# Pinning side work behind the instruction emitted ahead of it

## The chip, the cores and the metric

The kernel runs on one core of a Trainium2 chip. The core has five engines with one instruction queue each: TensorE (PE in the profile) for matrix products, VectorE (DVE) and ScalarE (ACT) for elementwise work, GpSimd (POOL) for a little of it, and SyncE (SP), which issues nearly all transfers. An engine works through its queue in order; between engines semaphores carry the waits. The metric is device time in microseconds (us) of one launch.

## The reference

One inference step of a hybrid decoder layer, for a prompt of 1024 tokens and for 8 sequences of 4 new tokens (32 "sample" rows), at width 1024:

```python
h = rmsnorm(x, g_norm) * (1 + scale) + shift              # shift, scale, gate from silu(c) @ w_ada
mq, mk, mv, mi, mf, mo, mz, aq, ak, av, az, gm, ga = split_in(h @ w_in)
y_m, C, n, m = mlstm_branch(mq, mk, mv, mi, mf, mo, mz, ...)   # 4 heads, chunks of 128, a 128x128 state C per head
q, k = partial_rope(aq), partial_rope(ak)
y_a = sliding_window_attention_with_sinks(q, k, av) * silu(az)  # 8 heads, 2 key/value heads, window 128
u = sigmoid(gm) * (y_m @ w_mo) + sigmoid(ga) * (y_a @ w_ao)
x = x + gate * (u @ w_o)                                   # then a last rmsnorm
```

Outputs are the normalised rows, the mLSTM states and the key/value caches of both parts, all in 32-bit floats.

## The kernel before, in words

Products are made at 32-bit precision from pairs: each operand is split into a high part (`..h`, `wh_..`, a cast on ACT) and a low part (`..l`, `wl_..`, a subtraction on DVE), and three products are added in PSUM. Large products go by a seven-product scheme on halves (`block_products`, `att_products`, `Rows`), whose operands are sums and differences of blocks (`t1` to `t4`, `s1`).

The main chain is written as a plain sequence of jobs: the first products of keys and values (`pair`), the queries (`queries`, whose evacuation `ev_q`, line 886, copies each piece out of PSUM on ACT as `aq`, applies rope on DVE and stores `aqr`), the first mLSTM projections (`head_jobs`), then `block_products` for the other projections and all gates, `att_products` for the attention's output product, the memory branch's output (`mem_out`) and the last product by rows (`Rows`).

Beside it run streams of side work, as Python generators: `unit` (line 814, one attention unit: scores, a maximum `mx`/`nmx`, exponentials, `den`, transposes `pt`, output `oT`), `gates` (596), `head` (1026: the mLSTM of one head, with `prep`, 1043, which masks the loaded `et` and scales `qw`, and `stage_b`, 1080, the chain of states C), `sample_head` (1160, which ends with two transposes `sty` and their evacuation `gs`), `sum_blocks` (1310, sums of the blocks of `x`), `ada_gate` (1917), `out_weights` (1941, products and sums of `w_out` rows, stored as `woD`) and `att_sums` (1587: loads `yr`, takes differences, splits them into `ym_l`/`ym_h` and `ya..`, the operands of `att_products`).

The class `Side` decides when a step of a stream is emitted. It keeps an estimate of PE's clock (`now`, moved on by every product), and after each product of the main chain `tick` steps every stream whose pause is over and whose PSUM bank is free. So the order in which instructions are emitted interleaves main and side work by planned times.

The order emitted isn't the order run. Products always keep it (`in_order`, on every `matmul` and `transpose`). `V`, `S` and `G` wrap VectorE, ScalarE and GpSimd; while `on` is true each of their instructions is tied to the one before it in its wrapper. From line 1913, where the first products are done, to line 2188, where the last rows begin, `V.on` and `S.on` are false, and the framework's scheduler may put an instruction of DVE or ACT ahead of others that were emitted before it, where data allow and where its own estimate says that it is ready earlier. A transfer is issued on SP in the order that the scheduler gives, behind what it waits for; a wait in a queue holds up everything behind it.

In the trace all wrapped instructions have line 220, products 259, transposes 264 and transfers 247; tiles tell them apart.

## Time and profile before

| | |
|---|---|
| median of 3 runs | 839.07 us (838.8 to 839.33) |
| profiled execution | 838.28 us, of which the span is 836.5 us |
| PE busy | 812.5 us, 97% |
| DVE busy | 595.0 us, 71% |
| ACT busy | 420.1 us, 50% |
| mean granted clock of PE | 0.993 |

The page names an instruction by line, engine, operation and "out<-in". A number in brackets at the end of a timeline row is the idle time of the engine just before it and what ended that; in the list of waits the three numbers are total, count and longest. Times are from the start of the span.

### The profile page before, as it was taken

Reading aid. Unit: us, or ns where it says so; the run is one execution under the profiler, and the core shown is the slowest. Engines: PE = TensorE matmul, PEld = TensorE weight load, DVE = VectorE, ACT = ScalarE, POOL = GpSimd, SP = SyncE. Lnnn points to the kernel's source line nnn. Section 1 sums busy time; section 2 is a strip of 40 time slices with the busy share of each in tenths; the row PEclk is TensorE's granted clock in tenths of the full one; section 3 lists DMA queues with packets and bytes.
Section 4 is the critical chain, followed back from the end, with each engine's and each line's share of the span. In section 5 each row is a group of like instructions: output and inputs, shape, how many; then the busy total and the mean of one; then the engine's idle time right before and its main releaser. Section 6 shows DMA issues by size and latency. Waiting matters only on the chain.

```text
span 836.5 us, 15032 instructions
## 1 busy us (share of the span) xinstructions
PE 812.5 (97%) x5129; PEld 670.9 (80%) x5129; DVE 595.0 (71%) x1479; ACT 420.1 (50%) x1030; POOL 67.4 (8%) x128
## 2 busy tenths in 40 slices
PE   6999999999999999999799999999999999999996
PEld 3779897888788788888688877787788789997775
DVE  4889886656655556475575886797668988974776
ACT  4664365655474564545445454444346654334343
POOL 0120000000000001000001010000002104250000
PEclk9999999999999999999899999999999999999998
DMA  9997766346436335388654354464236785643532
GB/s 337 373 356 233 203 188 201 118 156 210 140 111 196 104 107 174 112 271 292 228 175 167 106 178 138 156 203 141 99 93 191 239 291 180 214 134 131 201 107 108
DMA packets 106689, 153.96 MB, mean 184 GB/s; under 512 B 20448, under 2 KB 54368, under 8 KB 106580
## 3 DMA queue, kind: packets, MB, share of 16 engines
q1 hardware_dynamic: 100964, 142.25, 52.1%
q10 hardware_dynamic: 4176, 6.56, 2.3%
q0 software_dynamic: 1472, 4.20, 1.3%
q8 instruction: 40, 0.66, 0.3%
q14 instruction: 37, 0.30, 0.1%
HBM read 109.22 MB, written 44.75 MB: 184 GB/s over the span
## 4 chain that ended last, share of the span: by engine, by line
PE 91%; DVE 4%; DMA 2%; ACT 1%; issue 1%; SPq 1%; DVEq 0%; ACTq 0%
PE bx L259 11%; PE bw L259 11%; PE by L259 11%; PE g_aq L259 6%; PE bz L259 6%; PE g_w_mo L259 5%; PE g_mq L259 3%; PE foW L259 3%; PE foX L259 3%; PE foY L259 2%; PE smp L259 2%; PE oT L259 2%; PE foZ L259 2%; PE sc L259 2%; PE pt L264 2%; PE g_ak L259 1%
## 5 line engine op out<-in xcount | busy, mean ns | idle before, releaser
L220 ACT ACTIVATE p<-p,nmx 128x256 f32<-128x256 f32 (+1 forms) x64 | 31.0, 485 | 13.0 <-DVE nmx L220 12.7
L259 PE MATMUL g_aq<-h_h,wh_aq 128*128 128x384 f32 (+1 forms) x96 | 32.2, 336 | 0.0
L220 DVE CUSTOM_DVE_ANT_0 p<-sc,cst,sink 128x256 f32<-128x256 f32 (+1 forms) x64 | 26.2, 464 | 6.9 <-PE sc L259 6.8
L259 PE MATMUL g_aq<-h_h,wl_aq 128*128 128x384 f32 (+1 forms) x96 | 30.9, 322 | 0.0
L259 PE MATMUL g_aq<-h_l,wh_aq 128*128 128x384 f32 (+1 forms) x96 | 30.8, 321 | 0.0
L259 PE MATMUL g_w_mo<-ym_l,wh_w_mo 128*128 128x384 f32 (+1 forms) x96 | 30.8, 321 | 0.0
L259 PE MATMUL g_w_mo<-ym_h,wh_w_mo 128*128 128x384 f32 (+1 forms) x96 | 30.8, 321 | 0.0
L259 PE MATMUL g_w_mo<-ym_l,wl_w_mo 128*128 128x384 f32 (+1 forms) x96 | 30.8, 321 | 0.0
L247 POOL DMA_DIRECT2D oD<-uqv x16 | 8.9, 554 | 183.4 <-ACT uqv L220 183.4
L220 ACT ACTIVATE et<-et,an 128x128 f32<-128x128 f32 x32 | 11.2, 397 | 19.5 <-DVE et L220 19.3
L220 DVE COPY p<-pt 128x512 f32<-128x512 f32 (+1 forms) x16 | 10.5, 655 | 13.7 <-PE pt L264 13.7
L259 PEld LDWEIGHTS g_aq<-h_h,wh_aq 128*128 128x128 f32 x96 | 18.0, 188 | 2.6 <-issue 1.5
L259 PEld LDWEIGHTS g_w_mo<-ym_l,wh_w_mo 128*128 128x128 f32 x96 | 18.0, 188 | 0.0
L259 PEld LDWEIGHTS g_aq<-h_l,wh_aq 128*128 128x128 f32 x96 | 18.0, 188 | 0.0
L259 PEld LDWEIGHTS g_w_mo<-ym_h,wh_w_mo 128*128 128x128 f32 x96 | 18.0, 188 | 0.0
L259 PE MATMUL sc<-ukv,uqv 64*128 64x256 f32 (+1 forms) x128 | 18.0, 390 | 0.0
L259 PEld LDWEIGHTS g_w_mo<-ym_l,wl_w_mo 128*128 128x128 f32 x96 | 18.0, 188 | 0.0
L259 PEld LDWEIGHTS g_aq<-h_h,wl_aq 128*128 128x128 f32 x96 | 18.0, 188 | 0.0
L220 DVE TENSOR_TENSOR et<-et,cst 128x384 f32<-128x384 f32 (+1 forms) x12 | 6.1, 512 | 16.5 <-DMA et<-nmd 16.5
L264 PE MATMUL pt<-cst,p 128*128 128x128 f32 x120 | 16.4, 277 | 1.1 <-DVE mx L220 1.1
L259 PE MATMUL g_mq<-h_h,wh_mq 128*128 128x384 f32 (+1 forms) x48 | 16.8, 349 | 0.3 <-ACT mk L220 0.3
L220 ACT ACTIVATE sq<-rows_h 128x512 f32<-128x512 f32 (+2 forms) x14 | 8.2, 582 | 17.7 <-issue 12.0
(2073 smaller groups left out, 2848.0 us busy)
## 6 DMA issues: line engine op xcount, KB each, us to landing
x<-xT SPq DMA_DIRECT2D x16, 256.0 KB, 5.4
early_h<-w_ada SPq DMA_DIRECT2D x8, 512.0 KB, 9.1
adar_ga<-w_ada SPq DMA_DIRECT2D x16, 256.0 KB, 4.0
wr_ga<-w SPq DMA_DIRECT2D x16, 256.0 KB, 2.5
wr_gm<-w SPq DMA_DIRECT2D x16, 256.0 KB, 3.3
taD<-gt SPq DMA_DIRECT2D x16, 256.0 KB, 2.2
tmD<-gt SPq DMA_DIRECT2D x16, 256.0 KB, 4.8
wor<-w_out SPq DMA_DIRECT2D x16, 256.0 KB, 3.9
```

Of the source, the lines that this page charges most:

```text
L220: ins = f(*args, **kw)
L247: ins = (eng or nc.sync).dma_start(out, in_)
L259: in_order(nc.tensor.matmul(out, lhsT, rhs, start=start, stop=stop, skip_group_check=more))
L264: in_order(nc.tensor.transpose(out, in_, idn))
```

## The change

`Side.step` marks the two wrapped engines as `late` while a side stream emits a step. Each wrapper remembers the instruction that it emitted last (`before`), main or side. While `on` is false, an instruction emitted in a side step gets an order tie to that last one; an instruction of the main chain gets none. So a side instruction keeps its place behind the instruction emitted just ahead of it on its engine, and main instructions may still be moved ahead of others. GpSimd isn't in the list of engines.

```diff
     def step(self, item):
+        for e in self.engines:
+            e.late = True
         try:
             lag, banks = next(item[0])
             item[1:] = self.now + lag, banks
...
+        for e in self.engines:
+            e.late = False
...
             def __init__(self, eng, name):
-                self.eng, self.name, self.on = eng, name, True
+                self.eng, self.name, self.on, self.late, self.before = eng, name, True, False, None
...
                     ins = f(*args, **kw)
+                    i = getattr(ins, "ins", ins)
                     if self.on:
                         in_order(ins, self.name)
+                    elif self.late and self.before is not None:
+                        no_sync(i, [self.before])
+                    self.before = i
                     return ins
...
+        side.engines = V, S
```

More of the change, by code (lines that the diff above doesn't have):

```diff
@@ L118, in __init__ @@
     def __init__(self, each, limits, quiet):
-        self.each, self.free = each, {}
+        self.each, self.free, self.engines = each, {}, ()
         self.now, self.last, self.quiet, self.products = 0.0, 0.0, quiet, 0
```

## The prediction

> **What bounds the kernel now.** I read the page's first part, then PE's own waits, then a table of stretches, and last the instructions around each place that the change moves.

> ```profile
> span 836.5 us, 15032 instructions
> PE 812.5 (97%) x5129; PEld 670.9 (80%) x5129; DVE 595.0 (71%) x1479; ACT 420.1 (50%) x1030; POOL 67.4 (8%) x128
> ...
> PE xc L259 <- ACT xsq L220: 6.4, 1, 6.4
> PE S L259 <- DVE C L220: 5.5, 1, 5.5
> PE pt L264 <- DVE mx L220: 1.1, 1, 1.1
> ...
> 405.50:411.00 5.50, 0.04 (x2) 0.00 (x1) 1.44 (x4) 0.90 (x4) 0.00 (x0) 0.81 0.95 275
> 411.60:415.70 4.10, 4.10 (x12) 3.33 (x12) 2.67 (x6) 3.16 (x12) 0.10 (x1) 0.50 0.67 228
> 416.00:420.00 4.00, 4.00 (x47) 3.25 (x46) 2.17 (x4) 1.50 (x4) 0.00 (x0) 1.00 0.40 135
> ```

> PE is busy 97% of the span, so the time is PE's work plus PE's waits; what VectorE (DVE) and ScalarE (ACT) do costs nothing until PE waits for it. PE's list of waits shows one large one behind the start: 5.5 us, for DVE's C. In the table of stretches (columns: length, busy time of PE, its weight loads, DVE, ACT, POOL, then the granted clock, DMA share, GB/s) this wait has a second price: for the 4.1 us after it PE's clock is 0.50, which loses 4.1 x 0.5 = 2.05 us more. The span is 836.5 us, the profiled execution 838.28 us, and the median of the runs 839.07 us, 0.8 us more; I add what I find to the median.

> **What moves.** In the built order of the changed kernel PE and POOL have exactly the order of before. DVE, ACT and SP differ. A side instruction can no longer run ahead of what was emitted before it; a main instruction may still pass side work. So each effect is one of two: a side operation that used an early gap now stands late, or a main operation now stands in front of a side operation that PE needs. I went through the new DVE and ACT order with the durations and landings of the trace, and asked at each changed place when PE's operand would be there against when PE took it. Four places come out late or early by over 1 us.

> **Place 1, the query projections (106 to 123 us): costs 4.6 us.**

> ```profile
> 68.38 0.67 DVE L220 TENSOR_TENSOR x<-x,x 128x512 f32<-128x512 f32 x1
> ...
> 105.66 0.48 ACT L220 ACTIVATE aq<-g_aq 128x384 f32<-128x384 f32 x1
> 106.72 0.62 ACT L220 CAST wh_mq<-wr_mq 128x512 fp32r<-128x512 f32 x1 [0.57 <-PE g_aq L259]
> ...
> 106.65 0.34 PE L259 MATMUL g_aq<-h_h,wh_aq 128*128 128x384 f32 x1
> ...
> 110.52 0.12 DVE L220 TENSOR_TENSOR den<-den,nmx 128x4 f32<-128x4 f32 x1
> ...
> 111.84 0.17 DVE L220 TENSOR_TENSOR mr<-mr,row 1x32 f32<-1x32 f32 x1
> ...
> 111.65 0.91 ACT L220 ACTIVATE p<-p,den 128x256 f32<-128x256 f32 x2 [0.87 <-DVE den L220]
> 112.47 0.47 ACT L220 ACTIVATE aq<-g_aq 128x384 f32<-128x384 f32 x1
> ...
> 121.70 0.48 ACT L220 ACTIVATE aq<-g_aq 128x384 f32<-128x384 f32 x1
> ...
> 122.50 0.34 PE L259 MATMUL g_mq<-h_h,wh_mq 128*128 128x384 f32 x1
> ```

> First, on ACT, the second `wh_mq` cast now stands ahead of the `aq` copy of 105.66. The cast waits for PE to release its granule and begins at 106.72 whatever else happens, so the copy begins at about 107.26 (0.54 behind, the cast's 0.62 overlapping it a little): 1.6 us late, done at 107.74. PE needs the bank it frees at 106.65 and waits 1.1 us. Second, on DVE, the attention's `den` of 110.52 now stands behind the gate chain (`mr`, 111.84) and behind three dependent sums of `sum_blocks`, the `x` adds, which ran at 68 to 72 us and now come directly ahead of it. `mr` is itself 1.9 us late through the first step and ends near 113.9; three adds at 0.67 bring `den` to 115.9, 5.4 us late. On ACT the `p` scaling waits for `den` (the row names it) and the `aq` copy of 112.47 stands behind it, now near 117.6. The row of rope, score, exponential and `aq` copy that follows is a closed circle between the two engines and carries about 4.9 us on: the `aq` copy of 121.70 ends at 127.07 instead of 122.18. PE's first `g_mq` product takes that bank: 127.1 against 122.50, 4.6 us in all, the 1.1 us included (second stall about 3.45 us). No other work covers it, since PE's order is fixed. Until 165 us the later places are late by 4.2 us at most against PE's old times, so they disappear in this shift.

> Small ones in between: PE's 1.1 us wait for `mx` (at 291 us) is absorbed by the shift, and about +0.7 us appears near 191 us, where a copy of transposed `p` stands behind two sums of the blocks. I take -0.4 together (-1.5 to +1).

> **Place 2, the large wait: gains 3.9 us and the clock's 2.05 us.**

> ```profile
> 396.39 3.19 SPq L247 DMA_DIRECT2D woDb<-wor  x3
> ...
> 402.60 0.38 SPq L247 DMA_DIRECT2D hk<-kD  x1
> 403.51 0.42 SPq L247 DMA_DIRECT2D et<-nmd  x1
> ...
> 409.50 0.56 DVE L220 TENSOR_TENSOR et<-et,cst 128x384 f32<-128x384 f32 x1 [6.06 <-DMA et<-nmd]
> 410.12 0.56 DVE L220 TENSOR_TENSOR qw<-qw,hq 128x384 f32<-128x384 f32 x1
> 410.60 0.34 DVE L220 SCALAR_TENSOR_TENSOR C<-C,dec,U 128x129 f32<-128x129 f32 x1
> ...
> 411.00 1.22 PE L259 MATMUL S<-hq,hk 128*128 128x128 f32 x4 [5.46 <-DVE C L220]
> ```

> The third link of head 2's C chain stands behind head 3's `et`, which waits for its load; PE waits for the link to free a bank. In the changed order it still stands there: both are side work, emitted in that order. What moves is SP. Three stores of scaled `w_out` rows (`woDb`, 396.39 on, waiting for DVE's products) stood ahead of the head's loads; the products are now done later, their stores come behind these loads, and `et` is issued near 399.4 instead of 403.51, 4.1 us earlier. With the same 6.0 us to landing it is there at 405.4, the link ends near 406.9, and PE, which came at 405.54, waits about 1.4 us plus or minus: 5.5 - 1.4 = 4.1, of which I take 3.9 since place 1 shifts PE and DVE unequally. Such a short wait leaves the clock alone, so the 2.05 us go too. Bounds: the wait vanishes (-5.5 - 2.05 = -7.5), or the load lands as late against PE as before (0).

> **Place 3, the sample heads' transposes (586 us): costs 2.0 us.**

> ```profile
> 586.22 0.25 DVE L220 TENSOR_SCALAR gs<-sty,vec 128x32 f32<-128x32 f32 x1
> 586.39 0.68 DVE L220 TENSOR_TENSOR wl_phead_gate__6931<-ws,wh_phead_gate__6930 128x512 fp32r<-128x512 f32 x1
> 587.00 0.69 DVE L220 SCALAR_TENSOR_TENSOR hg<-hg,hg1z 128x512 f32<-128x512 f32 x1
> ...
> 587.78 0.68 DVE L220 TENSOR_TENSOR ws<-wr_mz,wr_mz 128x512 f32<-128x512 f32 x1
> ...
> 586.52 0.24 PE L264 MATMUL sty<-cst,sz 32*128 32x32 f32 x1 [0.77 <-DVE gs L220]
> ```

> PE's second `sty` waits for the first `gs`. Now three main operations stand ahead of `gs`: `wl_phead_gate`, `ws`, `hg`, at 0.61 from start to start (586.39 to 587.00). 3 x 0.61 = 1.8, and `ws` starts behind a wait for its operand: 2.0. PE has nothing else to do, its order being fixed. Between 1.8 and 2.1.

> **Place 4, the sums of the attention output (651 to 657 us): costs 3.4 us.**

> ```profile
> 651.34 0.68 DVE L220 TENSOR_TENSOR yr<-yr 128x512 f32<-128x512 f32 x1
> 651.95 0.68 DVE L220 TENSOR_TENSOR hg<-p,bw 128x512 f32<-128x512 f32 x1
> 652.54 1.19 DVE L220 TENSOR_TENSOR yr<-yr 128x512 f32<-128x512 f32 x1
> 653.65 0.68 DVE L220 TENSOR_TENSOR ym_h<-yr,ym_l 128x512 fp32r<-128x512 f32 x1
> ...
> 660.38 0.41 DVE L220 TENSOR_TENSOR wl_ao0C<-wr_ao,wh_ao0C 128x256 fp32r<-128x256 f32 x1
> 660.72 0.41 DVE L220 TENSOR_TENSOR wl_ao0D<-wr_ao,wh_ao0D 128x256 fp32r<-128x256 f32 x1
> ...
> 655.80 0.39 PE L259 MATMUL az<-ym_h,wh_ao0A 128*128 128x512 f32 x1
> 656.03 0.39 PE L259 MATMUL az<-ym_l,wl_ao0A 128*128 128x512 f32 x1
> 656.54 0.50 PE L259 MATMUL aw<-yat2h,wh_ao0B 128*128 128x512 f32 x1
> ```

> PE takes `ym_h` (a side product: `yr` difference, then split) at 655.80; it was ready at 654.33. Seven half-size main operations of the next weights (`wl_ao0B`, `wr_ao`, two `wl_ao0C`, a `ws`, two `wl_ao1A`) now run ahead of the `yr` of 651.34: 7 x 0.34 (660.38 to 660.72) = 2.4. Two `hg` operations that came behind and one that came behind the first `yr` add 3 x 0.6 = 1.8, and the queue is already 1.0 to 1.5 late here for the same reason. Together 5.2 for `ym_h`, which ends at 659.5: 3.7 us after 655.80. PE's old spacing of 0.51 at 656.54, against 0.23 before it, held 0.28 us of waiting that is absorbed: 3.4. From here PE runs without a gap to the output products, so all of it reaches the end. Bounds 1.5 (scheduling slack that I do not see) to 4.

> **The sum.** 4.6 - 0.4 - 3.9 - 2.05 + 2.0 + 3.4 = +3.6 us: 841.9 in the profile, 842.7 for the median.

> **Rivals.** (a) Place 2 gives nothing: the trace has DMA share 0.95 in that wait, so an earlier issue could land no sooner. Then +3.6 + 5.95 = +9.6, 848.6. Against it: half the wait was queueing on SP, which the rows show. (b) The clock falls at place 1. The 405.50:411.00 row has a mean of 0.81, so half the clock for 0.38 of 5.5 us: it fell 3.4 us after PE stopped. A stall of 3.45 us is on the edge of that, and would add up to 2.05: 844.8. [...] (c) Faster: side work has slack that swallows delays before they reach PE, at places 1 and 4, the only ones where the delay travels through several instructions. Place 1 then costs only its first step, 1.1, and place 4 its floor, 1.5: 1.1 - 0.4 - 5.95 + 2.0 + 1.5 = -1.75, 837.3. It decides if `den` comes less than 1.1 us late (0.32 us of margin lies between the `aq` copy's end at 122.18 and PE at 122.50, and 0.87 us of ACT's wait for `den` can be given up without harm if `p` comes later too). DVE's 71% speaks for it; against it, each link of the circle in the rows begins where the one before ends. (d) The moves cancel: place 1 at half its price, 840.4.

> **Chances.** Forecast 0.50 (840.8 to 845.5), (a) 0.12, (b) 0.13, (c) 0.12, (d) 0.13. A measurement of this kernel tells 0.2%, 1.7 us, from no change. Slower: forecast, (a), (b) and 0.02 of (d): 0.77. Within 0.2%: the rest of (d) and a third of (c): 0.15. Faster: the rest of (c): 0.08. The range, 838.5 to 847.5, leaves out (a) and (c).

> **What would show it.** Right: in PE's waits a line for `g_mq` behind ACT's `aq` of 3 to 4 us near 123 us; the wait of S for C under 2.5 us with the clock at full speed behind it; `sty` behind `gs` of 2.5 to 3 us in its longest; `az` behind `ym_l` or `ym_h` of 2 to 4 us. Wrong: no PE wait near 123 us, or the 5.5 us wait still there with its slow clock.

## The result and the profile after

The changed kernel takes 850.52 us, median of four runs (847.62 to 852.60), against 839.20 us (838.80 to 840.21) for the kernel before in the same comparison: 1.0131 times as long, 95% interval 1.0099 to 1.0162, so 11.3 us more. The profiled execution is the fastest of the four, 847.62 us with a span of 845.8 us; that of before took 838.28 us. The two traces therefore explain 9.3 us; the other 2 us lie in the runs that were not profiled, and come back below.

First the page of the changed kernel, then its list of TensorE's waits (total, number, longest).

```profile
span 845.8 us, 15020 instructions
PE 814.8 (96%) x5129; PEld 673.1 (80%) x5129; DVE 596.2 (70%) x1479; ACT 418.4 (49%) x1030; POOL 67.2 (8%) x128
...
PE xc L269 <- ACT xsq L224: 6.4, 1, 6.4
PE g_mq L269 <- ACT aq L224: 3.3, 1, 3.3
PE S L269 <- DVE C L224: 3.1, 1, 3.1
PE sty L274 <- DVE gs L224: 3.0, 2, 2.7
PE az L269 <- ACT ym_l L224: 2.2, 1, 2.2
PE sc L269 <- DVE p L224: 1.2, 1, 1.2
PE g_aq L269 <- ACT aq L224: 1.0, 1, 1.0
```

Busy times are those of before within 0.4%; what is new are waits, and half clock behind some of them. The four places of the forecast are all in this list: `g_mq` and `g_aq` (place 1), `S` (place 2, 5.5 us before), `sty` (place 3), `az` (place 4). What the forecast did not have stands in the table of stretches. These are the changed kernel's, cut at the edges of its half-clock stretches (columns as in the prediction; the seventh number is the granted clock).

```profile
124.72:128.13 3.41, 1.46 (x9) 1.16 (x11) 2.35 (x6) 2.36 (x8) 0.00 (x0) 1.00 0.80 257
128.13:131.54 3.41, 3.41 (x13) 2.84 (x10) 2.50 (x8) 1.36 (x4) 0.00 (x0) 0.50 0.65 223
196.40:199.81 3.41, 2.24 (x11) 1.34 (x11) 2.05 (x7) 0.78 (x3) 0.00 (x0) 1.00 1.00 320
199.81:203.22 3.41, 3.41 (x38) 2.73 (x37) 2.26 (x9) 0.76 (x2) 0.00 (x0) 0.50 0.83 245
411.44:414.85 3.41, 1.83 (x17) 1.59 (x15) 0.56 (x1) 1.73 (x8) 0.10 (x1) 1.00 0.65 221
414.85:418.26 3.41, 1.92 (x10) 1.68 (x11) 1.84 (x4) 1.17 (x4) 0.00 (x0) 1.00 0.71 251
418.26:421.68 3.42, 3.42 (x45) 2.79 (x43) 1.98 (x3) 2.21 (x5) 0.00 (x0) 1.00 0.72 253
588.93:592.34 3.41, 0.74 (x3) 0.62 (x4) 2.83 (x6) 0.92 (x2) 0.00 (x0) 1.00 0.00 0
592.34:595.75 3.41, 3.41 (x10) 2.62 (x9) 0.00 (x0) 0.00 (x0) 0.00 (x0) 0.50 0.00 0
```

After the waits of `g_mq`, `sc` and `sty` the clock is 0.50 for one stretch of 3.41 us each. After the 3.1 us wait of `S` it stays at 1.00. The slow stretches begin whole multiples of 3.413 us apart (199.81 - 128.13 = 71.68 = 21 x 3.413; 592.34 - 199.81 = 392.53 = 115 x 3.413): in this trace the edges lie on one grid, and the clock of a stretch goes with TensorE's busy time in the grid stretch ahead of it: 1.46 and 0.74 us of work were followed by 0.50. The wait of `S` is cut by an edge into two halves, each with over 1.8 us of work, and no slow stretch follows it. The stretch ahead of 199.81, with 2.24 us of work, does not fit this and is taken up at the end. Behind `az` the clock stayed at 1.00 as well, with 1.78 us of work in the stretch that holds most of the wait:

```profile
660.61:664.02 3.41, 1.78 (x8) 1.13 (x6) 3.38 (x7) 1.61 (x4) 0.51 (x1) 1.00 0.40 128
664.02:667.44 3.42, 2.64 (x10) 1.97 (x11) 3.35 (x5) 2.62 (x5) 1.10 (x1) 1.00 0.96 299
```

Laying each TensorE instruction's start in one trace beside its start in the other gives this account of the profiled executions, in us:

| where | forecast | measured |
|---|---|---|
| place 1, `g_aq` and `g_mq` | +4.6 | +4.6 |
| `sc` near 191 us / `mx` at 291 us | -0.4 together | +1.2 / -0.5 |
| place 2, wait of `S` | -3.9 | -2.5 |
| place 2, half clock that goes | -2.05 | -2.2 |
| place 3, `sty` | +2.0 | +1.9 |
| place 4, `az` | +3.4 | +2.5 |
| half clock behind `g_mq`, `sc`, `sty` | none | +1.6, +1.4, +1.5 |

The measured column sums to 9.5, within 0.2 of the 9.3. The other runs had still lower clocks: at 847.62, 850.41, 852.60 and 850.63 us the four were granted 0.991, 0.989, 0.987 and 0.989 of the full clock, which is at most 7.6, 9.3, 11.1 and 9.3 us lost ((1 - clock) x span, which also counts slow time in which TensorE waits). Three of these differ from the first by one or two stretches of 1.7 us (half of 3.41). The kernel before is granted 0.993 in most runs, 5.9 us lost. Of the 11.3 us between the medians some 3.4 (9.3 - 5.9) are clock and some 8 are waits; since the clock is on record to 0.001, or 0.85 us, this split is an estimate.

### The profile page after: what moved, and what is told of

Read it like the earlier page. It is cut to its first block, busy times and chain, and to the rows that moved or that the text cites. A ratio compares the mean times of both kernels' runs of the same rounds, so it can differ in the third digit from the quotient of the medians.

```text
span 845.8 us, 15020 instructions
## 1 busy us (share of the span) xinstructions
PE 814.8 (96%) x5129; PEld 673.1 (80%) x5129; DVE 596.2 (70%) x1479; ACT 418.4 (49%) x1030; POOL 67.2 (8%) x128
## 5 line engine op out<-in xcount | busy, mean ns | idle before, releaser
L224 ACT ACTIVATE p<-p,den 128x256 f32<-128x256 f32 (+1 forms) x32 | 14.2, 489 | 11.4 <-DVE den L224 11.4
L224 DVE TENSOR_TENSOR et<-et,S 128x384 f32<-128x384 f32 (+1 forms) x12 | 6.1, 510 | 15.9 <-PE S L269 14.3
```

Source lines behind the costliest of these rows:

```text
L224: ins = f(*args, **kw)
```

## The experiments

All ratios are to the kernel before, run beside each kernel on the same chip. In each diff, the lines are against the kernel named.

**One stage at a time.** Three kernels tie side work in one stage only: `first` until the first projections are done (`products_done`, at about 200 us), `gates` from there to the last query gate, `last` behind it. Against the changed kernel:

```
first:   products_done.append(True)
       + side.engines = ()
gates: - side.engines = V, S          (at the start; set behind products_done)
       + side.engines = ()
         def hook(n, i):
       +     if n == len(paired) + KT:
       +         side.engines = ()
last:  - side.engines = V, S          (at the start)
       + side.engines = ()
         def hook(n, i):
       +     if n == len(paired) + KT:
       +         side.engines = V, S
```

> Side work is tied only until the key/value products are done (to about 200 us); behind that it is free as before. Theory (the loss is made of single waits of TensorE, each with its stage, and of half-clock stretches that follow them): g_mq waits about 3.3 us behind aq, sc about 1.2 us behind p, two half-clock stretches of 3.4 us follow them at 1.5 us each, and the wait of S for C is the one of before, 5.5 us, with its two half-clock stretches: TensorE is 8 to 8.5 us late at 200 us and stays so, about +8 us to the kernel before (847). Rival (the loss is spread over the kernel by engines that hold each other up): about a quarter of the loss of 11 us, +3 us. Rival of the prediction's own sum (stalls without the clock): +5 to +6 us (845).

> Side work is tied only between the end of the key/value products and the end of the query gates (about 200 to 430 us). Theory: the only large change there is the wait of S for C, which falls from 5.5 to about 3.1 us, and the half-clock stretches behind it, worth 2.2 us, which go: -4.7 us to the kernel before (834.5), faster than both kernels. Rival (the clock falls behind any wait of 3 us): -2.5 to -3 us (836.5). Rival (the gain at this place came only because the earlier loss had already given C time): 0 us (839).

> Side work is tied only behind the query gates (from about 430 us). Theory: sty waits 2.7 us behind gs (+1.9), a half-clock stretch follows (+1.5), az waits some 2.4 us behind ym_l and ym_h: +5 to +6 us (845), with one half-clock stretch more than the kernel before. Prediction's own sum without the clock: +4 to +4.5 us (843.5). Rival (spread loss): +5.5 us too, but with many small waits in place of the two.

`first` took 848.41 us (1.0120, 1.0101 to 1.0138), `gates` 834.60 (0.9949, 0.9933 to 0.9966), `last` 846.46 (1.0099, 1.0078 to 1.0121), against 838.93. That is +9.5, -4.3 and +7.5, together +12.7 where the whole change costs 11.3; the difference is within the intervals, some 1.5 us on each term. The loss adds up from its stages, and in each of them TensorE's list has the waits named above and not many small ones. `gates` came near its expectation, though with one half-clock stretch left behind `S`, where none was expected. `first` and `last` each came out about 1.5 us or more above what was expected of them. The profiled execution of `last`, at 849.52 us the slowest of its four, shows what the clock can add:

```profile
659.87:663.28 3.41, 1.42 (x7) 0.74 (x5) 3.41 (x7) 1.41 (x3) 0.72 (x1) 1.00 0.42 127
663.28:666.70 3.42, 2.64 (x6) 1.82 (x7) 3.32 (x6) 2.83 (x5) 0.89 (x1) 0.50 0.87 280
666.70:670.11 3.41, 3.41 (x10) 2.65 (x9) 2.30 (x4) 0.89 (x2) 0.39 (x1) 0.50 0.84 301
```

Here place 4, whose `az` wait was 2.8 us and lay largely in one grid stretch (1.42 us of work), was followed by two slow stretches; in the changed kernel's profile the same wait had none. The other three runs of `last`, 846.04 to 846.70 us at a clock of 0.992 instead of 0.988, lost about two stretches less. So this does not explain why the median lies above the expectation; that stays open.

**What place 1 consists of.** `no_x` ties all streams but the block sums and attention sums. `skip_x` in addition does not tie other side work behind an instruction of that stream. Against the changed kernel:

```
no_x:   - e.late = True
        + e.late = item not in self.streams["x"]["live"]
skip_x: + if self.mark:               (False while a step of stream x runs)
        +     self.before = i
```

> All streams of side work are tied but that of the block sums and the attention sums (x). Theory: without the three block sums ahead of den the wait of g_mq behind aq shrinks from 3.3 us to 1 us or less and its half-clock stretch goes, sc behind p and az behind ym_l go; sty behind gs and its half-clock stretch stay (+3.4), S behind C keeps its gain (-4.7): 0 to +2 us to the kernel before (839 to 841), so 9 to 11 us under the changed kernel. Rival (the gate chain alone, not the block sums, makes g_mq late): g_mq still waits 2 to 3 us, +4 to +5 us.

> As no_x, and the other side work is not tied behind an instruction of the x stream either (it is tied behind the last one that is not of x). Theory (sc waits because the copy of p stands tied behind a block sum that waits for its load): the wait of sc for p and its half-clock stretch go, 1.5 + 1.3 us less than no_x, the wait of g_mq stays at about 1.8 us: 839 to 840. Rival (sc's wait comes from the order on ScalarE, where the scaling of p stands behind a copy of os): as no_x, 842.

`no_x` took 842.21 us (1.0045, 1.0026 to 1.0063) and `skip_x` 841.63 against 838.71 (1.0034, 1.0022 to 1.0047). In `no_x` TensorE is 2.0 us late at `g_mq` instead of 4.6 (its longest wait there is 1.8 us, where 1 or less was expected), `g_aq` no longer waits and `az` no longer waits: the ties of this stream make 2.6 us of place 1 (the sums ahead of `den`) and all of place 4 (the attention sums). The gate chain, most of which VectorE still runs ahead of the scaling of `p`, is the likely rest; no run frees it alone. The changed kernel's VectorE shows the chain that was forecast, with the three sums in one row:

```profile
113.22 0.18 DVE L224 TENSOR_TENSOR mr<-mr,row 1x32 f32<-1x32 f32 x1
113.33 2.12 DVE L224 TENSOR_TENSOR x<-x,x 128x512 f32<-128x512 f32 x3
115.37 0.15 DVE L224 TENSOR_TENSOR den<-den,nmx 128x4 f32<-128x4 f32 x1
```

`sc` still waited in `no_x`, against what was expected of it. On VectorE of `no_x`:

```profile
193.60 0.69 DVE L224 TENSOR_TENSOR hb<-hb,hb 128x512 f32<-128x512 f32 x1 [2.32 <-DMA wr_mq<-w]
194.21 0.55 DVE L224 COPY p<-pt 128x384 f32<-128x384 f32 x1
```

The copy of `p` is itself tied behind a block sum, which comes after 2.32 us of idle time; the releaser named is the transfer that the profile saw last. Freeing the sums alone does not free the copy. In `skip_x` the copy runs ahead of the sum and `sc` does not wait. So the place is the one the prediction named near 191 us, at 1.2 to 1.5 us instead of 0.7. The median fell by only 0.6 us, and not by the 2.8 expected: in the profiled execution of `skip_x` `g_mq` waits 2.3 us and the mean clock is 0.993, against 1.8 us and 0.995 in that of `no_x`, and the two intervals overlap.

**What place 2 consists of.** `pool` is the kernel before with the stores of the scaled `w_out` rows on POOL's queue; `g_only` is `gates` with only stream g tied.

```
pool:   - store(woD[name, k], t)
        + store(woD[name, k], t, nc.gpsimd)
g_only: - e.late = True
        + e.late = item in self.streams["g"]["live"]
```

> The kernel before, the stores of the scaled w_out rows moved from SP's queue to POOL's; the order on TensorE and ScalarE stays, on VectorE one wor product and one wl_pgate change places. Theory (the gain at 405 us comes from the three woDb stores that no longer stand ahead of the head's loads on SP): et<-nmd is issued some 3 to 4 us earlier, the wait of S for C falls to 2 to 3 us: -2.5 to -5 us (835 to 836.5). Rival (the gain comes from VectorE's or ScalarE's order, or the load lands no sooner because the DMA engines are full): the wait stays at 5 to 6 us, 0.

> In the same stage as gates (200 to 430 us), only the scaling of the w_out rows (stream g) is tied; all other side work is free as before. In the kernel before, five of its wor products run on VectorE at 394.5 to 399.2 us ahead of the main product gt, and SP's store taD waits for gt with the head's loads behind it. Theory (the gain at this place is that VectorE order: gt earlier, so the store and the loads behind it earlier): et<-nmd goes out some 3 us earlier against TensorE, the wait of S for C is 2.5 to 3.5 us and one half-clock stretch instead of two: -4 us (835), as gates. Rival (other side work's ties make the gain): 0 to -1 us.

`pool` took 840.92 us against 838.71 (1.0042, 1.0023 to 1.0060), with `S` waiting 6.1 us and a new wait of 1.2 us of `bw` for `ws`. `g_only` took 834.35 against 838.75 (0.9949, 0.9932 to 0.9967), as much as `gates`. The stores on SP were not what made the load late. In `pool`, first on VectorE and then on SP:

```profile
401.05 0.68 DVE L220 TENSOR_TENSOR gt<-p,bw 128x512 f32<-128x512 f32 x1
...
402.42 0.32 SPq L247 DMA_DIRECT2D taD<-gt  x1
...
405.44 0.42 SPq L247 DMA_DIRECT2D et<-nmd  x1
```

With the `woDb` stores gone, SP issues nothing from 397.1 to 402.42 us: it stands at the store of the main product `gt`, and `gt` comes late because VectorE runs four `wor` products of the side work ahead of it (four, not the five of the expectation). In the kernel before the same two rows lie at 399.15 (`gt`) and 400.53 us (`taD`), with `et` at 403.51. In `g_only` `gt` runs after one `wor`, at 397.13, and `et` is issued at 401.08 us:

```profile
397.13 0.68 DVE L224 TENSOR_TENSOR gt<-p,bw 128x512 f32<-128x512 f32 x1
...
406.95 0.56 DVE L224 TENSOR_TENSOR et<-et,cst 128x384 f32<-128x384 f32 x1 [3.24 <-DMA et<-nmd]
407.94 0.56 DVE L224 TENSOR_TENSOR qw<-qw,hq 128x384 f32<-128x384 f32 x1 [0.43 <-DMA qw<-wid]
```

**What the wait of `S` is made of.** `link` is the kernel before with `et` and `qw` ordered behind the last link of the C chain on VectorE; `gates_link` and `g_link` add the same to `gates` and `g_only`.

```
+ e = V.tensor_tensor(et[:, :m], et[:, :m], cmask..., op=ALU.add)
+ no_sync(getattr(e, "ins", e), links[-1:])
  ...                                           (the same for qw)
+ l = V.scalar_tensor_tensor(Cn, chain[-1], dec..., Un[:, i], ...)
+ links.append(getattr(l, "ins", l))
```

> The kernel before with one order more on VectorE: et and qw of a head come behind the last link of the C chain, so that the third link no longer stands behind a load. Theory (the wait of S for C is that link's place and nothing else): the wait of 5.5 us goes, and with it both half-clock stretches: -6.5 to -7.5 us (832). Rival (VectorE still stands at et until 409.5 us, and the next gate weights behind et come late now that TensorE comes earlier): a new wait of 2 to 4 us for a wl_pgate or for et, -3 to -5 us (835). Rival (S waits for the load in another way too): 0.

> gates with the order of link added: et and qw behind the last C link on VectorE. Theory (two costs in series at one place: the third link behind et, which link takes away, and the late load, which holds VectorE's et and ScalarE's exp with the copies behind it, which gates makes 3 us earlier): S no longer waits, the copies hv and hk come in time, no half-clock stretch: -7 to -8 us to the kernel before (831.5), 3 us under gates. Rival (the copies behind the exp are still late): smpo waits for hv 0.5 to 1.5 us, -5.5 to -6.5 us (833).

> g_only with the order of link added. Theory: as gates_link, -7 to -8 us (831.5), if g_only gives what gates gives. Rival: -3 us, as link alone.

`link` took 835.64 us (0.9962, 0.9948 to 0.9976): its rival's figure. `S` no longer waits, so the third link behind a load was indeed the whole wait. But `smpo` and `smp` now wait 1.6 and 1.4 us for ScalarE's copies `hv` and `hk`, which stand behind the exponential of the same late `et`:

```profile
409.67 0.40 ACT L220 ACTIVATE et<-et,an 128x128 f32<-128x128 f32 x1 [7.42 <-DVE et L220]
```

The 5.5 us wait had hidden that second queue. With both repaired, `gates_link` took 829.55 us (0.9889, 0.9874 to 0.9904), 2 us below what was expected of it, and `g_link` 831.32 (0.9920, 0.9896 to 0.9944), where `smp` still waits 1.1 us. TensorE's waits in `gates_link`, all over 0.2 us:

```profile
PE xc L269 <- ACT xsq L224: 6.8, 1, 6.8
PE sty L274 <- DVE gs L224: 1.1, 2, 0.8
PE adat_q L269 <- ACT adas_q L224: 0.7, 1, 0.7
PE xc L269 <- ACT xsum L224: 0.7, 1, 0.7
PE bw L269 <- ACT bw L224: 0.7, 1, 0.7
PE pt L274 <- DVE mx L224: 0.5, 1, 0.5
PE g_mq L269 <- ACT mk L224: 0.3, 1, 0.3
```

This kernel is 9.2 us faster than the kernel before and by the distances to it (9.2 and 11.3) some 20 us faster than the changed one.

**Place 3 by itself.** `swap` is the changed kernel with both `sty` transposes ahead of both `gs` products.

```
  for i, (g, _) in enumerate(tails):
      tr(ty[:, i], ns[:, i, 0:128], ident[:NS, :NS])
+ for i, (g, _) in enumerate(tails):
      V.tensor_scalar(gs[:, g], ty[:, i], gmn[:, g:g + 1], None, op0=ALU.mult)
```

> The changed kernel, with both sty transposes emitted ahead of both gs products, so that the second no longer waits for the first gs; nothing else moves. Theory: the 2.7 us wait and its half-clock stretch go, and nothing takes their place: TensorE gains 2.5 us against the changed kernel plus up to 1.5 us of clock: 847 to 848. Rival (gs is needed soon after by someone else): a wait of 1 to 2 us some us later, 849.5.

It took 846.41 us against 838.75 (1.0089, 1.0073 to 1.0105), 3.6 us less than the changed kernel by their medians' distances to the kernel before (7.7 against 11.3). `sty` is gone from TensorE's waits, and the runs were granted 0.989 to 0.993 of the clock, against 0.987 to 0.991 in the changed kernel's. No new wait took its place in that stage; `az` further on waited 2.8 us in the profiled execution, against 2.2 in the changed kernel's.

**The clock by itself.** `fill` is the changed kernel with nine products that nobody uses between the two `sty` transposes; `fill_S` is the kernel before with sixteen ahead of `S`.

```
fill:   + if h == 3 and not i:
        +     warm = po([128, 128], "warm")
        +     for _ in range(9):
        +         in_order(nc.tensor.matmul(warm, ident, ident, start=True, stop=True))
fill_S: + if h == 2 and p == 2:
        +     for _ in range(16):
        +         in_order(nc.tensor.matmul(tv[:, 2], ident, ident, start=True, stop=True))
```

> The changed kernel with nine products of a 128x128 unit matrix, used by nobody, on TensorE between the two sty transposes, where it waits 2.7 us for gs. The wait for gs ends at the same time. Theory (a half-clock stretch follows a stretch in which TensorE was idle too long): with TensorE busy in most of the wait no half-clock stretch follows at 590 us, so TensorE's lateness grows by 1.9 us there and not by 3.4: about 1.5 us less where the changed kernel has that stretch, 849 for the median. Rival (the slow clock comes from something else that goes on at this place, as the DMA traffic or the power drawn by what follows): the half-clock stretch is there as before, 850.5.

> The kernel before, with sixteen products of a unit matrix, used by nobody, on TensorE ahead of the S products, where it waits 5.5 us for C; they take about 4.0 us (9 took 2.27). Three instructions on ScalarE and VectorE behind change places. Theory (the half clock is set by TensorE's idle time in stretches of 3.41 us, and costs by itself): about 1.5 us of idle time stay, the wait ends at the same time, no half-clock stretch follows: the granted clock rises from 0.993 to 0.997 and the time falls by 1.8 to 2.1 us (836.8). Rival (what follows the wait is slow for another reason): the half clock stays, 0 (838.8).

In `fill` the products take 2.27 us of the wait, and the grid stretch that holds it and the one behind it both have the full clock:

```profile
591.89:595.30 3.41, 2.92 (x18) 2.38 (x17) 1.62 (x4) 0.00 (x0) 0.00 (x0) 1.00 0.00 0
595.30:598.72 3.42, 3.42 (x17) 2.84 (x16) 0.69 (x1) 0.62 (x1) 0.00 (x0) 1.00 0.03 5
```

The order of the work behind the wait is the same as in the changed kernel, so what follows the wait was not slow by itself. The median, 850.50 us (1.0141, 1.0113 to 1.0170), did not move, and the mean clock of the profiled execution is 0.990 against the changed kernel's 0.991: in it `S` waited 3.4 and `az` 2.8 us, against 3.1 and 2.2. That left the price open, and `fill_S` was made for it. There the median clock rose from 0.993 to 0.997 and the time fell to 837.89 us from 839.17 (0.9979, 0.9967 to 0.9990), 1.3 us and up to 2.8 by the interval, where 1.8 to 2.1 were expected. In its profiled execution one of the two slow stretches stayed, behind a grid stretch that still held 2.03 us of waiting:

```profile
408.70:412.11 3.41, 1.38 (x11) 1.15 (x10) 1.74 (x5) 2.33 (x10) 0.00 (x0) 1.00 0.92 341
412.11:415.52 3.41, 3.41 (x10) 2.62 (x9) 1.63 (x3) 1.17 (x4) 0.10 (x1) 0.50 0.80 251
415.52:418.94 3.42, 3.42 (x44) 2.78 (x44) 2.79 (x6) 2.71 (x7) 0.00 (x0) 1.00 0.55 193
```

## Why the prediction was wrong

The direction and the places were right; the size was not: 842.7 us was forecast and 850.52 measured, above the range's end of 847.5.

**Right.** Place 1 came at 4.6 us for 4.6, with `den` at 115.37 us between `mr` and the `aq` copies just as its rows were laid out (115.9 forecast). Place 3 came at 1.9 for 2.0, and `swap` removes it. The step of place 2 on what blocks `S` holds too: `link` shows that the third link behind `et` was the whole wait.

**The step that failed: the clock.** The sum has one clock term, the 2.05 us that go at place 2, and the sentence "Such a short wait leaves the clock alone". The limit behind it was read from a single row as 3.4 us of stopped TensorE (that wait began at 405.54 us, 0.08 behind an edge of the grid, and the clock fell at the next edge, 408.88), and waits of 2.0 to 3.45 us were priced as if nothing followed them, with rival (b) allowing one fall at place 1. In the profiled execution the clock fell behind waits of 3.3, 2.7 and 1.2 us, worth 1.4 to 1.6 us each. What decides, as far as the stretches shown here tell, is the busy time within one stretch of the grid. Those at full clock with 1.95 us or more of idle time were followed by half clock (1.95, 1.99, 2.03, 2.67, 2.84 idle: 0.50), and those with 1.86 us or less were not (1.58, 1.63, 1.86: 1.00), but for the one place named at the end. From these rows the bound is estimated near 1.9 us. A wait of 3 us is over it unless an edge cuts it near its middle. By this bound, three waits of 2.7 to 3.3 us and one of 2.2 should have carried about 1.5 us each for most positions of the grid. In the medians this is some +3.4 us of clock where -2.05 was forecast, about 5.5 of the 7.7 us that were missing.

That the 2.05 us at place 2 did go was luck. The wait left there was 3.1 us, not 1.4, and an edge halved it (1.58 and 1.49 us of idle time in the two stretches); in `gates` a wait of `S` of 2.9 us, 2.84 of idle time in one stretch, was followed by half clock.

**A term that was mis-sized: place 2.** It gave 2.5 us of wait instead of 3.9. The reason for the gain was wrong: the store that held SP was that of the main product `gt`, behind four side products on VectorE, not the `woDb` stores (`pool`, `g_only`). The size was off because only `et`'s load was followed. `qw` stands between `et` and the link, and its own load came later, by 1.27 us of VectorE's idle time in these rows of the changed kernel (no run tests it alone):

```profile
413.64 0.56 DVE L224 TENSOR_TENSOR et<-et,cst 128x384 f32<-128x384 f32 x1 [2.44 <-DMA tmD<-gt]
415.47 0.56 DVE L224 TENSOR_TENSOR qw<-qw,hq 128x384 f32<-128x384 f32 x1 [1.27 <-DMA qw<-wid]
415.95 0.34 DVE L224 SCALAR_TENSOR_TENSOR C<-C,dec,U 128x129 f32<-128x129 f32 x1
```

**Smaller ones.** The copy of `p` near 191 us cost 1.2 instead of 0.7 us; in `no_x` the sum ahead of it began only after idle time. Place 4 cost 2.5 instead of 3.4.

**The rivals.** (b) named the right term, and the clock did fall at place 1 (+1.6 us), but by a limit of 3.4 us without work that the runs do not bear out (1.95 us of idle time in the stretch were enough there), and at one place only. (a), (c) and (d) did not happen: place 2 gave most of its gain, and place 1 passed its delay on in full. The range was too narrow because no case let the clock fall more than once.

## What to carry to other kernels

Give a new wait on the engine that bounds the kernel two prices: its own length, and the clock behind it (here 1.4 to 1.6 us for a slow stretch), from the busy time in each stretch of the grid on which the profile's slow stretches lie; without the position of the grid, take the second as a chance and widen the range by its price for each such wait. When a load is late, follow its queue back to what the issue ahead of it waits for, and through the engine that makes that; a rule that holds back side work pays where side work ran ahead of a main product that a store or load waits for, and loses where the side work was itself on the path. When one wait is removed, look for the next queue that it hid: `link` alone gained 3.1 us, and 9.2 once the load was early as well (`gates_link`).

## What was not expected of the hardware

```profile
404.28:407.69 3.41, 0.57 (x6) 0.33 (x4) 1.38 (x3) 1.72 (x8) 0.10 (x1) 1.00 0.88 316
407.69:411.10 3.41, 3.39 (x10) 2.91 (x11) 1.02 (x2) 1.97 (x5) 0.00 (x0) 0.50 0.74 262
```

These are the two stretches of `gates`, with 2.84 us of idle time in the first; those of `g_only` follow, with 1.86 and 1.18:

```profile
404.22:407.64 3.42, 1.56 (x15) 1.32 (x13) 0.56 (x1) 0.10 (x1) 0.00 (x0) 1.00 0.78 224
407.64:411.05 3.41, 2.23 (x12) 1.93 (x13) 2.00 (x5) 3.38 (x14) 0.10 (x1) 1.00 0.77 278
```

Behind one stretch that was itself slow, less idle time was enough: in `last`, 663.28:666.70 has 2.64 us of work and 0.78 idle, and a second slow stretch follows. Taken at half clock these 2.64 us are by estimate 1.3 us of full-clock work, under the 1.5 us that the bound near 1.9 us leaves of 3.41. One place does not fit that bound: around 198 us, where in the changed kernel the stretch holds score products `sc` (1.73 us, operands of 64 rows) and three products of `g_mq` (0.59 us), 1.17 us of idle time were followed by half clock (0.50 at 199.81:203.22). What counts as busy there was not settled.
